# A two-layer attention trunk: q and k parts copied by DMA, dilated P scaled on ScalarE, differential P merged by one ratio

## The chip, the cores and the metric

The kernel runs on one core of a Trainium2 chip. The metric is device time in microseconds (us) of one execution. The core's engines are named as in the profile: PE (TensorE matmul), PEld (TensorE weight load), DVE (VectorE), ACT (ScalarE), POOL (GpSimd) and SP (SyncE, which here only issues DMAs). L12 is line 12 of the kernel before, unless another kernel is named.

## The reference

The input x is 512 tokens by 1024 channels, float32. There are two layers, each with the same parts:

```
h  = rms_norm(x) ;  u = h @ w_in                       # 1024 -> 10240
qa, ka, va, za, qb, kb, vb, zb, ga, gb = split(u)      # 1024 each
q, k of both branches: rotary turn of the first 16 of each head's 64 channels
branch A (16 heads of 64): softmax over three causal dilated windows, mixed by
    their softmax denominators                          # = one softmax with counts
branch B (8 heads, two q/k pairs of 64, v of 128):
    a = softmax(q1 k1) - lam * softmax(q2 k2) ; ob = rms_norm(a @ v) * (1 - lam_init)
ya = A * silu(za) ; yb = B * silu(zb)
x  = x + (sigmoid(ga) * (ya @ w_proj_a) + sigmoid(gb) * (yb @ w_proj_b)) @ w_out
```

A final rms_norm follows. All results are float32.

## The kernel before, in words

**Numbers.** Each float32 matrix product is made from two parts of each factor, a rounded high part and the remainder, and three matmuls: high by high, high by low, low by high. Whatever is to be multiplied is therefore first split, usually by one copy on ACT (the high part) and one subtraction on DVE (the low part). For the weights `split` (L99 to L103) does it, 1024 columns at a time.

**Projections.** Activations lie with channels on the 128 partitions and the 512 tokens along the row. `proj_T` (L268) makes one chunk of 256 output channels: 2 blocks `b` of 128, 8 steps `k` over the inputs, three 512-column matmuls per step (L282 to L284), into a PSUM tile `pj` of which there are three. At the end of a block an evacuation function is called. `proj_S` (L328) makes the two value projections of a layer with seven products instead of eight; its tiles X, Y, Z use the PSUM pools of scores, projections and transposes (two tiles, three and two).

**q and k.** A chunk ("qk", branch, u) holds 128 q channels (two heads, block 0) and the same 128 k channels (block 1). `ev_qk` (L398) evacuates a block: a shuffle on DVE (L401), a product with the cosine table on DVE (L403), a product with the sine table on POOL (L404), a sum on DVE (L405). Then the parts for the scores are made. The score matmuls (L480, L485, L486) contract over 128 partitions: 64 hold one part of a head's q, the other 64 the other part, and k is laid out so that two matmuls give all products. So each of the two heads needs its parts on both halves of the partitions; before, ACT and DVE write each half by instructions of 64 partitions by 512 columns (L410 to L413 for q, L419 to L422 for k).

**Dilated heads** (`a_pair`, L521, eight pairs a layer). For each half (one head): four score blocks (`s_steps`: matmuls, DVE adds the mask and takes the minimum at L487, ACT takes exp with its sum at L488); then `norm` multiplies the four blocks of 128, 256, 384 and 512 columns by the reciprocal sum on DVE (L528 to L531); `t_steps` transposes on PE (L506) and splits (L507 on ACT, L508 on DVE); `pv` multiplies with the values (L538).

**Differential heads** (`b_head`, L570, eight a layer). Two score maps P0 and P1 with their sums. `comb` (L575) forms P0/sum0 - lam * P1/sum1 with two DVE instructions per block (L582, L583). `pv` follows and collects the sums of squares (L605); after its second half the reciprocal root is taken (`inv_sqrt`, L238: DVE, then a power on POOL, L240), and four DVE instructions scale the output (L610); `turn` transposes it and multiplies with z (L618).

**z.** `ev_z` (L448) multiplies by the row scale `rb` on DVE (L453) and takes Silu on ACT. The first z chunk of a layer (`first`) runs before the row scales of the normalisation are known: at its last step `rstd_cols` and `layer_tables` make them, and then both blocks, which wait in the PSUM tiles of the scores, are evacuated (L287 to L291).

**Order.** Per layer: two z chunks, the value projection of A, the first q/k chunk, the value projection of B; then a merged list of `PARTS` (L886): chunks of q/k, z, the projection of A's result and the gates, with the steps of the heads laid between them by their nominal lengths (`merge`, L638). The steps of head u are paired with the value steps of head u-1 (`mix`). After that come the projection of B's result and the output projection. The instructions go to a planner in this order; it orders each engine's list by priority, which is the order of the program unless told otherwise, with a timing model for when operands and buffers are ready, and puts in all waits. Each engine then runs its list strictly in order.

**Buffers.** `b4` tiles (128 by 2 by 512) come from a pool of 29, which holds the normalised input, q and k parts, values, P, the branches' results and gates.

**DMA.** Weights come in chunks of 512 KB on SP's queue. POOL's queue carries 16 DMAs that add one half of a weight to another while loading (L112), all for the value projections. Values and projected results pass through device memory.

Of the kernel before, what the change touches and what calls it, by code (L numbers as in the profile page):

```python
# [16 lines left out]
P = 128  # L17
# [10 lines left out]
def bits(ap):  # L28
    return ap.bitcast(F32)
# [3 lines left out]
def trunk_kernel(ctx: ExitStack, tc: tile.TileContext, x, ws, norm_w, subln_w, final_w, lams, negb, rope, ident_in,  # L33
# [19 lines left out]
    def b4(name):  # L53
        return blk.tile([P, 2, T], F32R, tag="b4", name=name)
# [206 lines left out]
    def layer_tables():  # L261
        ps = rstd_rows()
        nc.scalar.activation(rb, ps, AF.Copy)
        nc.gpsimd.tensor_tensor(ct, rb, ct, OP.mult)
        nc.gpsimd.tensor_tensor(st, rb, st, OP.mult)


    def proj_T(what, rhs, evac, first=False):  # L268

        steps = []  # L270
        c, j0 = next_chunk(what)
        hold = {}

        def step(b, k):
            if b == 0 and k == 0:
                prep_to(j0 + 2)
            if k == 0:
                pool, tag = (pss, "s") if first else (psj, "pj")
                hold[b] = pool.tile([P, T], F32, tag=tag, name=f"pj{c}_{b}")
            ps, hb, o = hold[b], rhs(k), 256 * (k % 4) + b * P  # L280
            w_h, w_l = whi[j0 + k // 4][:, o:o + P], wlo[j0 + k // 4][:, o:o + P]
            nc.tensor.matmul(ps, w_h, hb[:, 0], start=(k == 0), stop=False)  # L282
            nc.tensor.matmul(ps, w_h, hb[:, 1], start=False, stop=False)  # L283
            nc.tensor.matmul(ps, w_l, hb[:, 0], start=False, stop=(k == 7))  # L284
            if b == 1 and k == 3:
                prep_to(j0 + 3)
            if k == 7 and first and b == 1:  # L287
                rstd_cols()
                layer_tables()
                for bb in range(2):  # L290
                    evac(bb, hold.pop(bb))  # L291
            if k == 7 and not first:
                evac(b, hold.pop(b))
        order = [(b, k) for k in range(8) for b in range(2)] if first else [(b, k) for b in range(2) for k in range(8)]
        for b, k in order:
            steps.append((683, lambda b=b, k=k: step(b, k)))
        return steps
# [97 lines left out]
    def hrhs(k):  # L395
        return st_["h"][k]

    def ev_qk(key):  # L398
        def f(b, ps):
            sw = t2(f"sw{key}{b}")  # L400
            nc.vector.stream_shuffle(sw, ps, SWAP)  # L401
            r = t2(f"rot{key}{b}")
            nc.vector.tensor_tensor(r, ps, ct, OP.mult)  # L403
            nc.gpsimd.tensor_tensor(sw, sw, st, OP.mult)  # L404
            nc.vector.tensor_tensor(r, r, sw, OP.add)  # L405
            lo, hi = slice(0, 64), slice(64, 128)
            if b == 0:
                qx = b4(f"qx{key}")

                nc.scalar.activation(qx[lo, 0], r[lo], AF.Copy, scale=-SCALE)  # L410
                nc.scalar.activation(qx[hi, 1], r[hi], AF.Copy, scale=-SCALE)
                nc.vector.scalar_tensor_tensor(qx[hi, 0], r[lo], -SCALE, bits(qx[lo, 0]), OP.mult, OP.subtract)
                nc.vector.scalar_tensor_tensor(qx[lo, 1], r[hi], -SCALE, bits(qx[hi, 1]), OP.mult, OP.subtract)  # L413
                st_["qk"][key] = [qx]
            else:

                for half, (mine, other) in enumerate(((lo, hi), (hi, lo))):
                    kx = b4(f"kx{key}{half}")
                    nc.scalar.activation(kx[mine, 1], r[mine], AF.Copy)  # L419
                    nc.vector.tensor_tensor(kx[mine, 0], r[mine], bits(kx[mine, 1]), OP.subtract)  # L420
                    nc.scalar.activation(kx[other, 0], bits(kx[mine, 1]), AF.Copy)
                    nc.vector.tensor_copy(kx[other, 1], bits(kx[mine, 0]))  # L422
                    st_["qk"][key].append(kx)
        return f

# [95 lines left out]
    def a_pair(layer, u):  # L521
# [4 lines left out]
        def norm(half):  # L526
            r = small.tile([P, 4], F32, tag="r", name=f"r{key}{half}")
            nc.vector.reciprocal(r, store["den", half])  # L528
            for i in range(4):
                p = store["p", half][i]  # L530
                nc.vector.tensor_scalar(p, p, r[:, i:i + 1], None, OP.mult)  # L531

        def pv(half):
            o = pso.tile([P, T], F32, tag="o", name=f"o{key}{half}")
# [35 lines left out]
    def b_head(layer, u):  # L570
# [2 lines left out]
        store = {}  # L573

        def comb():  # L575
            r = [small.tile([P, 4], F32, tag=f"rb{h}", name=f"rb{key}{h}") for h in range(2)]
            for h in range(2):
                nc.vector.reciprocal(r[h], store["den", h])
            nc.vector.tensor_scalar(r[1], r[1], nlam[:, layer:layer + 1], None, OP.mult)
            for i in range(4):  # L580
                p, p2 = store["p", 0][i], store["p", 1][i]
                nc.vector.tensor_scalar(p, p, r[0][:, i:i + 1], None, OP.mult)  # L582
                nc.vector.scalar_tensor_tensor(p, p2, r[1][:, i:i + 1], p, OP.mult, OP.add)  # L583

        def pv(half):

            ps = pso.tile([P, T], F32, tag="o", name=f"o{key}{half}")
            for n in range(2):
                i = 2 * half + n
                for j in range(i + 1):  # L590
                    v = store["v"][:, j]
                    for s in range(2):
                        nc.tensor.matmul(ps[:, 256 * n:256 * n + 256], pt_block(j, i, s), v,
                                         start=(j == 0 and s == 0), stop=(j == i and s == 1))
            if half == 0:
                store["o"] = tmp.tile([P, 4, P], F32, tag="t2", name=f"of{key}")
                store["ss"] = small.tile([P, 4], F32, tag="rs", name=f"rs{key}")
            o = store["o"][:, 2 * half:2 * half + 2]
            pp = ps.rearrange("p (n s d) -> p n s d", n=2, s=2)
            nc.scalar.activation(o, pp[:, :, 0], AF.Copy)  # L600
            nc.vector.tensor_tensor(o, pp[:, :, 1], o, OP.add)
            for n in range(2):
                i = 2 * half + n
                scr = small.tile([P, P], F32, tag="sqs", name=f"sqs{key}{i}", bufs=2)
                nc.scalar.activation(scr, o[:, n], AF.Square, accum_out=store["ss"][:, i:i + 1])  # L605
            if half == 1:
                r = store["ss"]
                inv_sqrt(r, r, 1.0 / P, 1e-5)
                for i in range(4):
                    nc.vector.tensor_scalar(store["o"][:, i], store["o"][:, i], r[:, i:i + 1], None, OP.mult)  # L610

        def turn():
            ps = pst.tile([P, T], F32, tag="t", name=f"ot{key}")
# [17 lines left out]
        def values(half):  # L631
            if half == 0:
                return t_steps((key, 0), store, 0) + [(900, lambda: pv(0)), (900, lambda: pv(1))]
            return [(430, turn)]
        return scores, values


# [356 lines left out]
```

## Time and profile before

| | |
|---|---|
| median of 3 runs | 1426.5 us (1426.38 to 1427.1) |
| the profiled execution | 1429.07 us |
| its span, first to last instruction | 1427.3 us |
| busy: PE, DVE, ACT, POOL | 1376.5, 1102.9, 879.0, 166.5 us |
| mean granted clock of TensorE | 0.989 |

A busy time is the union of an engine's instructions; instructions that only wait or issue on a queue are not in it. A group row of the profile has the line, the engine, the operation, output and inputs, shape, the count, then busy us and the mean ns of one, then idle time just before them and what ended it. A wait row has who waited, for whom, and us in total, times, longest. A timeline row has start us, length us, engine, line, and in brackets the idle time before it.

### The profile page before, as it was taken

What the parts mean: (1) busy time and instruction counts of PE and PEld (TensorE: products, weight loads), DVE (VectorE), ACT (ScalarE), POOL (GpSimd) and SP (SyncE); (2) the same over time, 40 slices, a digit from 0 to 9 for tenths busy, and PEclk for the clock granted to TensorE, in tenths of its full rate; (3) what the DMA queues carried; (4) which work ended last, traced back from release to release, by engine and by line L of the source; (5) the groups of instructions that cost most, each with busy time, mean ns of one, the idle gap of its engine ahead of it and who ended that gap; (6) DMA issues with size and microseconds to landing.
All of it is one profiled execution on the core that took longest, in us unless ns stands there. A gap on an engine that the chain in (4) does not pass through costs nothing.

```text
span 1427.3 us, 19038 instructions
## 1 busy us (share of the span) xinstructions
PE 1376.5 (96%) x6728; PEld 1144.1 (80%) x6728; DVE 1102.9 (77%) x2252; ACT 879.0 (62%) x1630; POOL 166.5 (12%) x139
## 2 busy tenths in 40 slices
PE   7999999999999999999999999999999999999998
PEld 5788777878788888888878887777878888888898
DVE  6876999999967898645466879999998688975554
ACT  8665667667665668632566666667766567774333
POOL 4100110110101120110220011010110011111000
PEclk9999999999999999999999999999999999999999
DMA  9643222212233323333585242212223322243421
GB/s 300 166 118 118 78 86 65 75 54 82 70 118 101 95 91 110 110 108 103 182 266 132 60 133 82 63 64 82 68 73 96 123 92 85 86 125 94 165 90 66
DMA packets 64607, 152.57 MB, mean 107 GB/s; under 512 B 6016, under 2 KB 22528, under 8 KB 64512
## 3 DMA queue, kind: packets, MB, share of 16 engines
q1 hardware_dynamic: 45312, 134.57, 29.4%
q0 software_dynamic: 2304, 8.39, 3.3%
q10 hardware_dynamic: 16896, 8.39, 2.0%
q8 instruction: 53, 0.87, 0.2%
q14 instruction: 42, 0.34, 0.1%
HBM read 134.55 MB, written 16.78 MB: 106 GB/s over the span
## 4 chain that ended last, share of the span: by engine, by line
PE 67%; DVE 19%; issue 7%; ACT 5%; DMA 1%; POOL 1%; SPq 0%; POOLq 0%; DVEq 0%; ACTq 0%
PE pj L282 16%; PE pj L283 16%; PE pj L284 16%; DVE wlo L103 3%; DVE pt L508 2%; PE X L303 1%; PE X L304 1%; PE X L302 1%; PE pv L302 1%; PE pv L304 1%; PE pv L303 1%; ACT whi L102 1%; DMA T<-ws_d 1%; PE Y L303 1%; POOL sq L206 1%
## 5 line engine op out<-in xcount | busy, mean ns | idle before, releaser
L282 PE MATMUL pj<-h,whi 128*128 128x512 f32 x1024 | 410.1, 402 | 15.0 <-DVE whi L801 6.5
L283 PE MATMUL pj<-h,whi 128*128 128x512 f32 x1024 | 408.0, 398 | 1.2 <-DVE h L189 1.1
L284 PE MATMUL pj<-h,wlo 128*128 128x512 f32 x1024 | 405.6, 398 | 0.0
L102 ACT ACTIVATE whi<-raw 128x1024 fp32r<-128x1024 f32 x207 | 218.7, 1057 | 173.2 <-PE pj L283 114.2
L103 DVE TENSOR_TENSOR wlo<-raw,whi 128x1024 fp32r<-128x1024 f32 x207 | 258.5, 1249 | 83.0 <-ACT whi L102 82.7
L282 PEld LDWEIGHTS pj<-h,whi 128*128 128x128 f32 x1024 | 195.5, 191 | 59.5 <-issue 6.4
L284 PEld LDWEIGHTS pj<-h,wlo 128*128 128x128 f32 x1024 | 195.3, 191 | 39.2 <-DVE wlo L103 0.3
L283 PEld LDWEIGHTS pj<-h,whi 128*128 128x128 f32 x1024 | 195.3, 191 | 39.1 <-DVE h L189 2.9
L103 DVE TENSOR_TENSOR wlo<-T,whi 128x1024 fp32r<-128x1024 f32 x24 | 31.2, 1300 | 14.9 <-ACT whi L102 14.8
L696 POOL TENSOR_TENSOR g<-g,pr 128x512 f32<-128x512 f32 x16 | 21.2, 1326 | 148.0 <-ACT g L695 148.0
L303 PE MATMUL pv<-wlo,mg 128*128 128x256 f32 x128 | 35.7, 283 | 0.0
L304 PE MATMUL pv<-whi,mg 128*128 128x256 f32 x128 | 35.7, 283 | 0.0
L302 PE MATMUL pv<-whi,mg 128*128 128x256 f32 x128 | 35.4, 283 | 0.0
L704 DVE TENSOR_TENSOR g<-pj,g 128x512 f32<-128x512 f32 x16 | 11.1, 692 | 30.5 <-PE pj L284 30.5
L102 ACT ACTIVATE whi<-T 128x1024 fp32r<-128x1024 f32 x24 | 25.1, 1055 | 8.6 <-PE pj L283 2.9
L206 POOL TENSOR_TENSOR sq<-sq,sq 128x512 f32<-128x512 f32 x12 | 19.7, 1638 | 88.6 <-issue 53.4
L708 ACT ACTIVATE mg<-g 128x512 fp32r<-128x512 f32 x16 | 10.1, 632 | 29.5 <-DVE g L705 29.5
L488 ACT ACT_TABLE_LOAD x21 | 26.9, 1283 | 0.3
L302 PE MATMUL X<-whi,h 128*128 128x512 f32 x64 | 24.1, 402 | 2.5 <-DVE z(0, 0, 0)_292 L453 2.5
L693 DVE TENSOR_TENSOR g<-pj,rb 128x512 f32<-128x512 f32 x32 | 22.0, 686 | 5.7 <-PE pj L284 5.6
L303 PE MATMUL X<-wlo,S 128*128 128x512 f32 x64 | 25.1, 393 | 0.8 <-DVE wlo L103 0.8
L303 PE MATMUL Y<-wlo,S 128*128 128x512 f32 x64 | 25.0, 391 | 0.8 <-DVE wlo L103 0.8
(4176 smaller groups left out, 3279.9 us busy)
## 6 DMA issues: line engine op xcount, KB each, us to landing
raw<-ws_d SPq DMA_DIRECT2D x199, 512.0 KB, 3.7
T<-ws_d POOLq DMA_DIRECT2D x16, 512.0 KB, 7.5
v_dram<-c ACTq DMA_DIRECT2D x24, 256.0 KB, 2.6
pa_dram<-pa SPq DMA_DIRECT2D x16, 256.0 KB, 3.1
pr<-pa_dram SPq DMA_DIRECT2D x16, 256.0 KB, 4.0
v_dram<-v ACTq DMA_DIRECT2D x8, 256.0 KB, 5.9
xr<-x_d SPq DMA_DIRECT2D x8, 256.0 KB, 4.4
x_dram<-xr SPq DMA_DIRECT2D x8, 256.0 KB, 3.2
```

What stands on the lines that cost most here:

```text
L102: nc.scalar.activation(whi[j], src, AF.Copy)
L103: nc.vector.tensor_tensor(wlo[j], src, bits(whi[j]), OP.subtract)
L206: nc.gpsimd.tensor_tensor(st_["acc"], st_["acc"], s, OP.add)
L282: nc.tensor.matmul(ps, w_h, hb[:, 0], start=(k == 0), stop=False)
L283: nc.tensor.matmul(ps, w_h, hb[:, 1], start=False, stop=False)
L284: nc.tensor.matmul(ps, w_l, hb[:, 0], start=False, stop=(k == 7))
L302: nc.tensor.matmul(ps, hh, w_h, start=first, stop=False, skip_group_check=True)
L303: nc.tensor.matmul(ps, hh, w_l, start=False, stop=False, skip_group_check=True)
L304: nc.tensor.matmul(ps, hl, w_h, start=False, stop=last, skip_group_check=True)
L488: nc.scalar.activation(p, p, AF.Exp, bias=mn[:, i:i + 1], scale=-1.0, accum_out=den[:, i:i + 1])
L508: nc.vector.tensor_tensor(dst[:, 1], ps[:, :n], bits(dst[:, 0]), OP.subtract)
L693: nc.vector.tensor_tensor(g[:, b], ps, rb, OP.mult)
```

## The change

Four edits, all in the functions above.

1. `ev_qk` no longer writes the halves by ACT and DVE. It makes one tile `hl` per block: the high part of all 128 partitions with one ACT copy, the low part with one DVE instruction. DMAs issued by POOL (`move`) then put the 64-partition pieces where the score matmuls want them: four for q (128 KB each), six for k (two of 256 KB, four of 128 KB).
2. `norm` of the dilated heads multiplies on ACT instead of DVE.
3. `comb` of the differential heads keeps P0 as it is and adds P1 times the ratio -lam * sum0/sum1, one DVE instruction a block. The missing factor 1/sum0 comes back as the scale of the squares (L605) and in the scaling of the output, which becomes one DVE instruction of 512 columns; root and scaling become steps of their own ahead of `turn`.
4. The row scales and the evacuation of the first z chunk are planned at high priority.

```
 proj_T:
             if k == 7 and first and b == 1:
-                rstd_cols()
-                layer_tables()
-                for bb in range(2):
-                    evac(bb, hold.pop(bb))
+                with tc.high_priority():
+                    rstd_cols()
+                    layer_tables()
+                    for bb in range(2):
+                        evac(bb, hold.pop(bb))
...
+    def move(to, of):
+        nc.gpsimd.dma_start(bits(to), bits(of))
 ev_qk:
+            hl = b4(f"hl{key}{b}")
+            f_ = -SCALE if b == 0 else 1.0
+            nc.scalar.activation(hl[:, 1], r, AF.Copy, scale=f_)
+            nc.vector.scalar_tensor_tensor(hl[:, 0], r, f_, bits(hl[:, 1]), OP.mult, OP.subtract)
             if b == 0:
                 qx = b4(f"qx{key}")
-                nc.scalar.activation(qx[lo, 0], r[lo], AF.Copy, scale=-SCALE)
-                nc.scalar.activation(qx[hi, 1], r[hi], AF.Copy, scale=-SCALE)
-                nc.vector.scalar_tensor_tensor(qx[hi, 0], r[lo], -SCALE, bits(qx[lo, 0]), OP.mult, OP.subtract)
-                nc.vector.scalar_tensor_tensor(qx[lo, 1], r[hi], -SCALE, bits(qx[hi, 1]), OP.mult, OP.subtract)
+                for half in range(2):
+                    mine = slice(64 * half, 64 * half + 64)
+                    move(qx[0:64, half], hl[mine, 1])
+                    move(qx[64:128, half], hl[mine, 0])
             else:
-                for half, (mine, other) in enumerate(((lo, hi), (hi, lo))):
+                for half in range(2):
                     kx = b4(f"kx{key}{half}")
-                    nc.scalar.activation(kx[mine, 1], r[mine], AF.Copy)
-                    nc.vector.tensor_tensor(kx[mine, 0], r[mine], bits(kx[mine, 1]), OP.subtract)
-                    nc.scalar.activation(kx[other, 0], bits(kx[mine, 1]), AF.Copy)
-                    nc.vector.tensor_copy(kx[other, 1], bits(kx[mine, 0]))
+                    mine = slice(64 * half, 64 * half + 64)
+                    move(kx[0:64], hl[mine])
+                    move(kx[64:128, 0], hl[mine, 1])
+                    move(kx[64:128, 1], hl[mine, 0])
...
 norm (a_pair):
-                nc.vector.tensor_scalar(p, p, r[:, i:i + 1], None, OP.mult)
+                nc.scalar.activation(p, p, AF.Copy, scale=r[:, i:i + 1])
...
 comb (b_head):
-            r = [small.tile([P, 4], F32, tag=f"rb{h}", name=f"rb{key}{h}") for h in range(2)]
-            for h in range(2):
-                nc.vector.reciprocal(r[h], store["den", h])
-            nc.vector.tensor_scalar(r[1], r[1], nlam[:, layer:layer + 1], None, OP.mult)
+            r = small.tile([P, 4], F32, tag="rb0", name=f"rb{key}")
+            q = small.tile([P, 4], F32, tag="rb1", name=f"rq{key}")
+            nc.vector.reciprocal(q, store["den", 1])
+            nc.vector.reciprocal(r, store["den", 0])
+            nc.vector.scalar_tensor_tensor(q, q, nlam[:, layer:layer + 1], store["den", 0], OP.mult, OP.mult)
+            store["r"] = r
             for i in range(4):
                 p, p2 = store["p", 0][i], store["p", 1][i]
-                nc.vector.tensor_scalar(p, p, r[0][:, i:i + 1], None, OP.mult)
-                nc.vector.scalar_tensor_tensor(p, p2, r[1][:, i:i + 1], p, OP.mult, OP.add)
+                nc.vector.scalar_tensor_tensor(p, p2, q[:, i:i + 1], p, OP.mult, OP.add)
...
 pv (b_head):
-                nc.scalar.activation(scr, o[:, n], AF.Square, accum_out=store["ss"][:, i:i + 1])
-            if half == 1:
-                r = store["ss"]
-                inv_sqrt(r, r, 1.0 / P, 1e-5)
-                for i in range(4):
-                    nc.vector.tensor_scalar(store["o"][:, i], store["o"][:, i], r[:, i:i + 1], None, OP.mult)
+                nc.scalar.activation(scr, o[:, n], AF.Square, scale=r, accum_out=store["ss"][:, i:i + 1])
+        def rms():
+            r = store["ss"]
+            inv_sqrt(r, r, 1.0 / P, 1e-5)
+        def scale():
+            r = store["ss"]
+            nc.vector.tensor_tensor(r, r, store["r"], OP.mult)
+            o = store["o"]
+            nc.vector.tensor_tensor(o, o, r.unsqueeze(2).to_broadcast([P, 4, P]), OP.mult)
...
-            return [(430, turn)]
+            return [(0, rms), (0, scale), (430, turn)]
```

More of the change, by code (lines that the diff above doesn't have):

```diff
@@ L405, in f @@
             nc.vector.tensor_tensor(r, r, sw, OP.add)
-            lo, hi = slice(0, 64), slice(64, 128)
+            hl = b4(f"hl{key}{b}")
+            f_ = -SCALE if b == 0 else 1.0
+            nc.scalar.activation(hl[:, 1], r, AF.Copy, scale=f_)
+            nc.vector.scalar_tensor_tensor(hl[:, 0], r, f_, bits(hl[:, 1]), OP.mult, OP.subtract)
             if b == 0:
                 qx = b4(f"qx{key}")
-                nc.scalar.activation(qx[lo, 0], r[lo], AF.Copy, scale=-SCALE)
-                nc.scalar.activation(qx[hi, 1], r[hi], AF.Copy, scale=-SCALE)
-                nc.vector.scalar_tensor_tensor(qx[hi, 0], r[lo], -SCALE, bits(qx[lo, 0]), OP.mult, OP.subtract)
-                nc.vector.scalar_tensor_tensor(qx[lo, 1], r[hi], -SCALE, bits(qx[hi, 1]), OP.mult, OP.subtract)
+                for half in range(2):
+                    mine = slice(64 * half, 64 * half + 64)
+                    move(qx[0:64, half], hl[mine, 1])
+                    move(qx[64:128, half], hl[mine, 0])
                 st_["qk"][key] = [qx]
             else:
-                for half, (mine, other) in enumerate(((lo, hi), (hi, lo))):
+                for half in range(2):
                     kx = b4(f"kx{key}{half}")
-                    nc.scalar.activation(kx[mine, 1], r[mine], AF.Copy)
-                    nc.vector.tensor_tensor(kx[mine, 0], r[mine], bits(kx[mine, 1]), OP.subtract)
-                    nc.scalar.activation(kx[other, 0], bits(kx[mine, 1]), AF.Copy)
-                    nc.vector.tensor_copy(kx[other, 1], bits(kx[mine, 0]))
+                    mine = slice(64 * half, 64 * half + 64)
+                    move(kx[0:64], hl[mine])
+                    move(kx[64:128, 0], hl[mine, 1])
+                    move(kx[64:128, 1], hl[mine, 0])
                     st_["qk"][key].append(kx)
@@ L603, in pv @@
                 i = 2 * half + n
+                r = store["r"][:, i:i + 1]
                 scr = small.tile([P, P], F32, tag="sqs", name=f"sqs{key}{i}", bufs=2)
-                nc.scalar.activation(scr, o[:, n], AF.Square, accum_out=store["ss"][:, i:i + 1])
-            if half == 1:
-                r = store["ss"]
-                inv_sqrt(r, r, 1.0 / P, 1e-5)
-                for i in range(4):
-                    nc.vector.tensor_scalar(store["o"][:, i], store["o"][:, i], r[:, i:i + 1], None, OP.mult)
+                nc.scalar.activation(scr, o[:, n], AF.Square, scale=r, accum_out=store["ss"][:, i:i + 1])
[7 more added lines that the diff above has]
+            nc.vector.tensor_tensor(o, o, r.unsqueeze(2).to_broadcast([P, 4, P]), OP.mult)
         def turn():
```

## The prediction

> **What bounds the kernel now.** I read the page first, then a table of five stretches, then PE's waits. The page:
>
> ```profile
> span 1427.3 us, 19038 instructions
> PE 1376.5 (96%) x6728; PEld 1144.1 (80%) x6728; DVE 1102.9 (77%) x2252; ACT 879.0 (62%) x1630; POOL 166.5 (12%) x139
> ```
>
> PE is busy 96% of the span, so at first sight there are only 51 us to win. But PE's busy time flatters: a 512-column matmul is shown with some 400 ns, while a clean stretch starts one every 222 ns (90 in 20 us), so a short stall disappears inside the neighbour's modelled length. The weight loads (PEld, one for each matmul) are the better measure of work done. The table by stretches (columns: stretch, length, then busy time and count of PE, PEld, DVE, ACT, POOL, then granted clock, DMA share, GB/s):
>
> ```profile
> 40.00:60.00 20.00, 18.56 (x75) 15.20 (x76) 16.02 (x28) 12.65 (x16) 0.89 (x1) 0.91 0.58 160
> ...
> 160.00:400.00 240.00, 225.62 (x1090) 183.42 (x1089) 223.68 (x518) 164.03 (x331) 24.37 (x19) 0.98 0.24 73
> ...
> 420.00:620.00 200.00, 199.04 (x997) 167.16 (x996) 153.07 (x353) 128.92 (x270) 25.16 (x21) 1.00 0.32 102
> ...
> 860.00:1100.00 240.00, 226.54 (x1095) 185.14 (x1094) 225.04 (x519) 164.16 (x330) 24.77 (x19) 0.97 0.25 76
> ...
> 1120.00:1320.00 200.00, 199.04 (x997) 167.15 (x996) 153.09 (x348) 127.23 (x267) 26.55 (x22) 1.00 0.32 100
> ```
>
> 160 to 400 us is the dilated branch of layer 0 with the first differential heads, 860 to 1100 the same of layer 1; there **DVE is 93% and 94% busy**, PE idles 14.4 and 13.5 us and the granted clock falls to 0.98 and 0.97. 420 to 620 and 1120 to 1320 are the differential heads: DVE 77%, PE idle under 1 us. Loads per us are 167.16/200 = 0.836 in the second kind and 183.42/240 = 0.764 and 185.14/240 = 0.771 in the first. At 0.836 the work of the dilated stretches would take 183.42/0.836 = 219.5 and 221.5 us: **20.5 and 18.5 us are lost, 39 together**. The mixes differ, so this is an estimate; its floor is the visible idle, 28 us. PE's waits name DVE:
>
> ```profile
> PE X L302 <- DVE z(0, 0, 0)_292 L453: 2.5, 1, 2.5
> PE o(1, 0, 0)1_7678 L538 <- DVE pt L508: 2.3, 1, 2.3
> ...
> PE pj L282 <- DVE rot(1, 0, 4)1_7988 L403: 1.2, 1, 1.2
> ```
>
> The dilated stage is therefore bound by DVE's queue, the rest by PE. An edit pays if it takes DVE work out of that stage.
>
> **The change, part by part.** What the removed instructions cost over the whole run; rows in this order: on DVE L412, L413 (q), L420, L422 (k), L531 (dilated normalisation), L582 and L610 (differential heads), then on ACT L410, L411, L419, L421. Columns as above with the one engine alone:
>
> ```profile
> 0.00:1427.30 1427.30, 21.92 (x32) 0.99 0.35 107
> 0.00:1427.30 1427.30, 24.34 (x32) 0.99 0.35 107
> 0.00:1427.30 1427.30, 45.40 (x64) 0.99 0.35 107
> 0.00:1427.30 1427.30, 29.80 (x64) 0.99 0.35 107
> 0.00:1427.30 1427.30, 42.66 (x128) 0.99 0.35 107
> 0.00:1427.30 1427.30, 21.23 (x64) 0.99 0.35 107
> 0.00:1427.30 1427.30, 16.00 (x64) 0.99 0.35 107
> 0.00:1427.30 1427.30, 19.95 (x32) 0.99 0.35 107
> 0.00:1427.30 1427.30, 20.18 (x32) 0.99 0.35 107
> 0.00:1427.30 1427.30, 40.31 (x64) 0.99 0.35 107
> 0.00:1427.30 1427.30, 40.46 (x64) 0.99 0.35 107
> ```
>
> And the nearest rows for what comes instead:
>
> ```profile
> L189 DVE SCALAR_TENSOR_TENSOR h<-xr,nw,h 128x512 fp32r<-128x512 f32 x8 | 6.0, 746 | 1.6 <-ACT h L188 1.6
> L708 ACT ACTIVATE mg<-g 128x512 fp32r<-128x512 f32 x16 | 10.1, 632 | 29.5 <-DVE g L705 29.5
> L429 ACT ACTIVATE c<-c,rstd 128x512 f32<-128x512 f32 x24 | 15.9, 711 | 0.7 <-DVE c L352 0.6
> L605 ACT ACTIVATE sqs(0, 1, 0)0_3481<-of(0, 1, 0)_3477 x1: 297/297/297, 399.3 to 399.3; 128x128 f32<-128x128 f32 x1
> L112 POOL DMA_DIRECT2D T<-ws_d x16 | 14.3, 916 | 55.4 <-ACT T L111 49.2 <-PE X L304 5.9 <-DVE S3f L225 0.3
> ```
>
> *q and k parts.* There are 32 q/k chunks. DVE per chunk: out 121.46/32 = 3.80 us, in two 128x512 subtractions at 0.746, so -2.30. ACT: out 120.9/32 = 3.78, in two at 0.632, so -2.51. Ten chunks fall into a dilated stretch: DVE -23.0, ACT -25.1 us.
>
> *Dilated normalisation.* Four DVE instructions per half head, 42.66/32 = 1.33 us, go to ACT. With a per-partition scale ACT takes 0.711 at 512 columns; at 128 columns I take 0.297 plus the 0.08 that separates 711 from 632, so 0.38; four widths average 0.545, 2.18 us a half. Fifteen halves per stretch: DVE -20.0, ACT +32.7. No table load comes with it, since the copies of L429 and L708 carry none.
>
> *Differential merge.* L582 goes: 21.23/16 = 1.33 us a head on DVE. L610's four multiplies (1.00 us a head) become one 128x512 (between 0.69 and 0.75) and a four-column one. Two merges fall into a stretch, -2.7; the other heads stand where DVE is only 77% busy and PE hides it: nothing.
>
> So a dilated stretch's DVE goes from 223.7 to 223.7-23.0-20.0-2.7 = **178**, its ACT from 164.0 to **171.6**. On a stretch of 220 us that is 81% and 78%: both near the 77% at which the differential stretch loses nothing, not at it. I give back a tenth of the 39 us, 4. Then PE's own work is late next.
>
> *The moves.* Each chunk adds 4 + 6 DMAs, issued on POOL. L112 is the only issue of that kind in the trace: 0.92 us, so 9.2 us a chunk; with two multiplies of 1.3 POOL gets 11.8 us a chunk, in a stretch of ten chunks 118 of 220. Landing is not shown for copies inside the chip's memory; bounds:
>
> ```profile
> T<-ws_d POOLq DMA_DIRECT2D x16, 512.0 KB, 7.5
> v_dram<-c ACTq DMA_DIRECT2D x24, 256.0 KB, 2.6
> ```
>
> A move carries 128 or 256 KB and adds nothing up, so 4 us, nearer the lower. From the end of the rotation to the first score a head then needs 0.63 + 0.75 + three issues (2.75) + 4 = 8.1 us. What it has, in the first and in the tightest case:
>
> ```profile
> 148.59 0.68 DVE L405 TENSOR_TENSOR rot(0, 0, 1)1_1232<-rot(0, 0, 1)1_1232,sw(0, 0, 1)1_1230 128x512 f32<-128x512 f32 x1
> ...
> 160.14 0.28 PE L480 MATMUL s(0, 0, 1)00_1265<-kx(0, 0, 1)0_1236,qx(0, 0, 1)_1159 128*128 128x256 f32 x1
> ```
> ```profile
> 516.75 0.68 DVE L405 TENSOR_TENSOR rot(0, 1, 6)1_4750<-rot(0, 1, 6)1_4750,sw(0, 1, 6)1_4748 128x512 f32<-128x512 f32 x1
> ...
> 524.75 0.28 PE L480 MATMUL s(0, 1, 6)00_4924<-kx(0, 1, 6)0_4754,qx(0, 1, 6)_4665 128*128 128x256 f32 x1
> ```
>
> 10.9 and 7.3 us. The same two rows of all 32 heads give 7 to 12 us for nine of them (mean 10) and over 15 for the others. So the tightest loses a little: 1 us a layer, 2 together. What hides the rest is projection matmuls between. Behind a move that waits for its source on POOL stand the next chunk's L404 multiply, for which L405 and then the PSUM tile wait, and in the differential heads L240's power; a chunk has over 20 us, so I cost that at nothing (if the cover goes: the rival below). Two more tiles of the 29-buffer pool live a few us per chunk; at nothing for the same reason.
>
> *A rule that speaks against it.* POOL's issue and DVE's work do overlap in the trace, and an elementwise POOL instruction does hold DVE:
>
> ```profile
> 29.01 1.28 DVE L225 TENSOR_TENSOR S3f<-x 128x512 f32<-128x512 f32 x2
> 29.36 1.83 POOL L112 DMA_DIRECT2D T<-ws_d  x2
> ```
> ```profile
> 210.34 1.28 POOL L404 TENSOR_TENSOR sw(0, 0, 4)1_1776<-sw(0, 0, 4)1_1776,st 128x512 f32<-128x512 f32 x1 [10.82 <-DVE sw(0, 0, 4)1_1776 L401]
> 210.81 1.36 DVE L413 SCALAR_TENSOR_TENSOR qx(0, 0, 4)_1686<-rot(0, 0, 4)0_1682,qx(0, 0, 4)_1686 64x512 fp32r<-64x512 f32 x1
> ```
>
> Two issues under two DVE additions: neither is longer (0.92 each, 1.28 for two). Under L404 a DVE instruction took 1.36, where the mean of its 32 is 24.34/32 = 0.76. So an elementwise POOL instruction costs DVE time and an issue costs it nothing here. The Trainium skill, "SBUF — State Buffer", section "SBUF: two separate sides", says that a DMA issued from POOL cannot write its descriptors while DVE runs a copy or a tensor-scalar in its two-port mode, and tells of a 620 ns transfer that took 3100 ns. By that an issue waits for such a DVE instruction and the time is that of rival (c), 1445; of these forms, though, L422, L531, L582 and L610 go with the change, and by the row above the sum stays.
>
> *First z.* PE's 2.5 us wait for L453, in the 40 to 60 stretch with the clock at 0.91:
>
> ```profile
> 33.38 0.58 ACT L263 ACTIVATE rb<-ps_rb 128x512 f32<-128x512 f32 x1
> ...
> 40.70 1.28 DVE L453 TENSOR_TENSOR z(0, 0, 0)_292<-pj,rb 128x512 f32<-128x512 f32 x2
> ...
> 41.44 0.50 PE L302 MATMUL X<-whi,h 128*128 128x512 f32 x1 [2.52 <-DVE z(0, 0, 0)_292 L453]
> ```
>
> Its scale is ready at 34.0 and DVE takes it at 40.7 behind other work. Put ahead, the 2.5 go, and some of the clock (20 x 0.09 = 1.8); the work now pushed back 1.3 us feeds PE too. Between 0 and 4.3; I take 3.
>
> **Sum.** 39 - 4 - 2 + 3 = 36, and 1 for the stretches' edges: 37. The profiled execution took 1429.07 us (span 1427.3 and 1.8 around it), 2.6 above the median 1426.5. 1429.07 - 37 - 2.6 = **1389.5, say 1390 us**.
>
> **Rivals.** (a) *ACT becomes the bound.* Normalisation now stands in ACT's queue between exp and the transposes, 0.85 us longer per half than on DVE and behind 1.06 us weight splits. For it: ACT at 78% serves PE's PSUM copies too. Against: it also loses 25 us. If each of 32 halves makes PE wait 0.6 us, 19 come back: 1409. (b) *PE's order, not DVE, sets the stage.* For it: PE's 96%, and single waits of 1 us and less. Against: two stretches of like work whose loss follows DVE's share. Then only z is won: 1424. (c) *Slower: the moves come late.* If an issue doubles to 1.8 us, as L413 did under L404, landing is 7.5 and one of q's moves still stands in front, a head needs 1.4 + 4 x 1.8 + 7.5 = 16.1 us; the nine tight heads lose 6.1 each, 55: 1390 + 55 = 1445. It decides from about 14.4 us a head on, where nine times 4.4 eats up the 37 and 2.9 more. For it: 320 issues where there were 16. Against: the 0.92 and the 2.6 rows. (d) *The change doesn't take DVE work out*, because L404 and the new 128-partition instructions hold each other; it is (b)'s time.
>
> **Numbers.** Forecast 58%, (a) 20, (b) with (d) 10, (c) 10, better than the range 2. The likeliest's own range: 1375 to 1402. The stalls hidden in PE's modelled length may be half as much again as the 39, so 58 won: 1429.07 - 58 - 3 - 2.6 = 1366, the low end. The high end takes in (a) and (b): 1424. A change under 0.2% (2.9 us) can't be told from none. Faster 0.80, same 0.09, slower 0.11.
>
> **What would show it.** Right: DVE under 85% and PE's loads above 0.82 a us in the dilated stretches, which end some 18 us earlier each; L112-like issues near 0.9 us, landing under 5; no wait of X for L453. Wrong: PE waits for kx or for a DMA at L480 (c), for ACT's p or pt (a), or DVE at 75% with PE's loads still at 0.77 (b).

## The result, and the profile after

| | before | after |
|---|---|---|
| median of 4 runs each on one chip | 1426.8 us (1426.38 to 1429.17) | 1391.96 us (1391.43 to 1392.57) |
| the profiled execution, its span | 1429.07, 1427.3 | 1392.57, 1390.8 |
| mean granted clock of TensorE | 0.989 | 0.994 |

The change takes 34.8 us: a ratio of 0.9753, 95% interval 0.9736 to 0.977. The forecast was 1390, with 37 us to be won. Line numbers from here on are those of the kernel after: the moves are issued at L400, the sine product is L408, the two halves `hl` are made at L415 (ACT) and L416 (DVE), `ev_z` multiplies at L461, the first score matmul is L488, the dilated normalisation is L539, and `t_steps` has L514 (PE), L515 (ACT) and L516 (DVE).

The page of the kernel after, its first lines and the queue that carries the moves (packets, MB, share of 16 engines):

```profile
span 1390.8 us, 19560 instructions
...
PE 1356.6 (98%) x6728; PEld 1138.8 (82%) x6728; DVE 971.6 (70%) x1900; ACT 859.2 (62%) x1630; POOL 335.7 (24%) x459
...
q0 software_dynamic: 19712, 58.74, 18.8%
```

DVE lost 131 us of work, ACT only 20, POOL gained 169; nearly all of that, 166.56 us, is the issuing of the moves, which does count in POOL's busy time. The table by stretches of the kernel after, with the columns of the prediction's first table; the second dilated stretch is read 20 to 40 us earlier, where its work now lies:

```profile
40.00:60.00 20.00, 19.01 (x77) 15.55 (x78) 15.99 (x28) 13.07 (x17) 0.88 (x1) 0.91 0.55 153
...
160.00:400.00 240.00, 236.14 (x1190) 197.75 (x1189) 192.36 (x436) 176.24 (x379) 76.19 (x118) 0.99 0.56 148
420.00:620.00 200.00, 200.00 (x993) 168.07 (x992) 133.12 (x276) 116.05 (x228) 47.67 (x61) 1.00 0.48 136
820.00:1080.00 260.00, 254.44 (x1281) 213.25 (x1280) 207.66 (x469) 189.15 (x405) 83.86 (x130) 0.99 0.57 149
1120.00:1320.00 200.00, 200.00 (x988) 167.54 (x988) 131.49 (x260) 112.88 (x211) 40.02 (x49) 1.00 0.45 134
```

In the dilated stretches PE's loads come at 197.75/240 = 0.824 and 213.25/260 = 0.820 a us, where they came at 0.764 and 0.771; DVE is 80% busy in both (192.36/240, 207.66/260), ACT 73% in both. The differential stretches run at 168.07/200 = 0.840 and 0.838, hardly above their 0.836.

Where the time came from is read by work done at fixed times. Weight loads alone (busy us and count), before:

```profile
0.00:400.00 400.00, 302.35 (x1726) 0.98 0.37 110
400.00:800.00 400.00, 332.15 (x1900) 1.00 0.42 128
800.00:1100.00 300.00, 234.27 (x1364) 0.98 0.26 80
```

and after:

```profile
0.00:400.00 400.00, 317.81 (x1835) 0.99 0.60 164
400.00:800.00 400.00, 332.32 (x1887) 1.00 0.50 143
800.00:1100.00 300.00, 246.86 (x1473) 0.99 0.55 147
```

By 400 us the kernel after is 317.81 - 302.35 = 15.46 us of loads ahead, and from 800 to 1100 it gains another 12.59; between, nothing (0.17). At 0.836 a us that is 18.5 us won in the dilated stretch of layer 0, 0.2 between and 15.1 in layer 1, 33.8 of the 36.5 us by which the span fell. But the busy time of the loads isn't quite a fixed measure either: the same 6728 loads take 1144.1 us before and 1138.8 after. Their number is fixed, so the time at which the n-th load starts places the whole difference (us from the start of the span):

| load | before | after | lead of after |
|---|---|---|---|
| 560th | 143.45 | 142.30 | 1.2 |
| 1680th | 389.61 | 368.76 | 20.9 |
| 3640th | 803.94 | 781.53 | 22.4 |
| 5040th | 1110.00 | 1070.04 | 40.0 |
| 6728th, the last | 1420.45 | 1379.58 | 40.9 |
| end of the span | 1427.26 | 1390.79 | 36.5 |

So 19.7 us are won in the dilated stretch of layer 0 and 17.6 in that of layer 1, 3.6 in all other stretches together, and **4.4 us are lost again behind the last load**. What differs there is a DRAIN instruction of POOL at the end of the program (the three drains of this line, shortest, median and longest in ns, before and after):

```profile
L989 POOLq DRAIN  x3: 40/102/1979, 1422.5 to 1427.0; - x3
```
```profile
L1005 POOLq DRAIN  x3: 46/93/8342, 1381.7 to 1390.5; - x3
```

The longest takes 8.34 us where it took 1.98, and the span ends 0.8 us behind it (before, 2.8 us). In all ten kernels of this record with ten moves a chunk on POOL's queue it takes 8.34 us, in the three without moves there 1.97 or 1.98. With twenty half moves a chunk it takes 4.84, so it doesn't simply grow with their number; why is open.

What PE waits for, the longest lines of the kernel after:

```profile
PE pj L282 <- DVE whi L817: 6.5, 1, 6.5
PE X L303 <- DVE z(0, 0, 0)_292 L461: 2.5, 1, 2.5
PE s(1, 0, 2)00_7759 L488 <- DMA kx(1, 0, 2)0_7658<-hl(1, 0, 2)1_7655: 1.7, 1, 1.7
```

The 2.3 us waits of `o` for `pt` are gone. A single head waits 1.7 us for a move. The wait of X for the first z is the same 2.5 us as before.

### The profile page after: what moved, and what is told of

Read it like the earlier page. It is cut to its first block, busy times and chain, and to the rows that moved or that the text cites. A ratio compares the mean times of both kernels' runs of the same rounds, so it can differ in the third digit from the quotient of the medians.

```text
span 1390.8 us, 19560 instructions
## 1 busy us (share of the span) xinstructions
PE 1356.6 (98%) x6728; PEld 1138.8 (82%) x6728; DVE 971.6 (70%) x1900; ACT 859.2 (62%) x1630; POOL 335.7 (24%) x459
## 4 chain that ended last, share of the span: by engine, by line
PE 91%; DVE 3%; DMA 2%; ACT 1%; issue 1%; POOL 1%; SPq 0%; POOLq 0%; DVEq 0%; ACTq 0%
PE pj L282 21%; PE pj L283 21%; PE pj L284 21%; PE X L304 2%; PE X L305 2%; PE X L303 2%; PE Y L304 1%; PE Y L305 1%; PE Y L303 1%; PE pv L303 1%; PE pv L305 1%; PE pv L304 1%; DMA T<-ws_d 1%; DMA kx(1, 0, 2)0_7658<-hl(1, 0, 2)1_7655 1%; DVE wlo L103 1%
## 5 line engine op out<-in xcount | busy, mean ns | idle before, releaser
L103 DVE TENSOR_TENSOR wlo<-raw,whi 128x1024 fp32r<-128x1024 f32 x207 | 264.8, 1280 | 103.8 <-ACT whi L102 103.3
L206 POOL TENSOR_TENSOR sq<-sq,sq 128x512 f32<-128x512 f32 x12 | 19.7, 1642 | 88.1 <-ACT sq L202 87.7
L103 DVE TENSOR_TENSOR wlo<-T,whi 128x1024 fp32r<-128x1024 f32 x24 | 29.3, 1224 | 15.2 <-ACT whi L102 15.1
L720 DVE TENSOR_TENSOR g<-pj,g 128x512 f32<-128x512 f32 x16 | 11.1, 692 | 30.5 <-PE pj L284 30.5
L102 ACT ACTIVATE whi<-T 128x1024 fp32r<-128x1024 f32 x24 | 25.2, 1056 | 10.8 <-DVE T L134 3.9
L112 POOL DMA_DIRECT2D T<-ws_d x16 | 14.6, 930 | 53.9 <-ACT T L111 43.3
L304 PE MATMUL X<-wlo,h 128*128 128x512 f32 x64 | 25.8, 403 | 0.4 <-DVE wlo L103 0.4
```

What stands on the lines that cost most here:

```text
L102: nc.scalar.activation(whi[j], src, AF.Copy)
L103: nc.vector.tensor_tensor(wlo[j], src, bits(whi[j]), OP.subtract)
L206: nc.gpsimd.tensor_tensor(st_["acc"], st_["acc"], s, OP.add)
L304: nc.tensor.matmul(ps, hh, w_l, start=False, stop=False, skip_group_check=True)
```

## The experiments

Each kernel ran on the same chip as a set of runs of the kernel before, whose median was 1426.8 to 1428.05 us; kernels are therefore compared by their ratios to it, and a difference of two ratios is turned into us at 1427. One interval is about plus or minus 2 us wide.

One thing is common to all of them. The planner makes new lists for each kernel: the matmuls are the same 6728, but 734 to 1287 of them stand at another place of PE's list than in the kernel after (111 with edit 4 undone), counted as those outside the longest part in common order. No run kept the order fixed, so a difference is that of the edit and of the new order together. A new order can be cheap: edit 3 undone moves 734 matmuls and costs nothing that can be told.

| kernel | median us | ratio to before (95%) | against after |
|---|---|---|---|
| after | 1391.96 | 0.9753 (0.9736 to 0.977) | |
| edit 1 undone | 1421.45 | 0.9962 (0.9947 to 0.9976) | +29.8 |
| edit 2 undone | 1394.31 | 0.9772 (0.9758 to 0.9787) | +2.7 |
| edit 3 undone | 1390.58 | 0.9746 (0.9731 to 0.976) | -1.0 |
| edit 4 undone | 1392.43 | 0.9759 (0.9742 to 0.9775) | +0.9 |
| DVE work added back | 1420.88 | 0.9945 (0.9929 to 0.9962) | +27.4 |
| ACT work added back | 1399.49 | 0.9802 (0.9787 to 0.9817) | +7.0 |
| both added back | 1418.13 | 0.993 (0.9911 to 0.9949) | +25.3 |
| moves in two | 1449.97 | 1.0153 (1.0138 to 1.0168) | +57.1 |
| moves on SP's queue | 1408.52 | 0.9874 (0.9847 to 0.9902) | +17.3 |
| norm on DVE, copy on ACT | 1456.47 | 1.0207 (1.0188 to 1.0226) | +64.8 |
| norm on ACT, copy on DVE | 1471.45 | 1.0312 (1.0298 to 1.0326) | +79.8 |
| first z put ahead by an edge, edit 3 undone | 1389.44 | 0.9736 (0.9723 to 0.9749) | -2.4 |

### Each edit undone

Edit 1 undone: `ev_qk` makes the halves by ACT and DVE as before, edits 2 to 4 stay.

```diff
-            hl = b4(f"hl{key}{b}")
-            nc.scalar.activation(hl[:, 1], r, AF.Copy, scale=f_)
-            nc.vector.scalar_tensor_tensor(hl[:, 0], r, f_, bits(hl[:, 1]), OP.mult, OP.subtract)
-            ... ten moves ...
+            # L410 to L413 and L419 to L422 of before
```

> The changed kernel with its first edit undone: the parts of q and k are again written by ACT and DVE instructions of 64 partitions, and no tile is moved by DMA. DVE theory (the dilated stretches were lengthened by DVE's queue): DVE gets 2.3 us a chunk back, 23 us in each dilated stretch, so its share there goes from 80% to some 90%, and about half of the 35 us come back: 1403 to 1414 us, PE's loads per us there near 0.79. Rival (the moves bring little and their lateness costs): the time stays at 1392 or falls to 1388, with DVE's share up and PE's loads per us unchanged.

1421.45 us: neither expectation held; nearly all of the gain, 29.8 of 34.8 us, goes with this one edit. By the count of loads it loses 15.8 and 15.1 us in the two dilated stretches, and wins the 4.4 us back at the end, since no move is on POOL's queue. Two windows of 220 us inside the dilated stretches, in the columns of the tables by stretches, for before, after and this kernel:

```profile
160.00:380.00 220.00, 206.91 (x1000) 168.37 (x999) 204.80 (x470) 148.08 (x293) 24.37 (x19) 0.98 0.23 69
840.00:1060.00 220.00, 207.41 (x1010) 169.60 (x1010) 206.53 (x472) 151.30 (x299) 23.71 (x19) 0.98 0.23 71
```
```profile
160.00:380.00 220.00, 216.15 (x1090) 181.17 (x1089) 178.26 (x404) 161.97 (x346) 75.15 (x117) 0.99 0.58 150
840.00:1060.00 220.00, 214.44 (x1081) 179.81 (x1080) 177.19 (x402) 161.04 (x343) 74.15 (x115) 0.99 0.57 147
```
```profile
160.00:380.00 220.00, 208.42 (x1026) 171.72 (x1024) 189.34 (x417) 177.90 (x361) 24.43 (x19) 0.99 0.23 72
840.00:1060.00 220.00, 210.42 (x1038) 174.00 (x1037) 190.38 (x422) 182.11 (x370) 26.04 (x21) 0.98 0.23 72
```

DVE stands at 86 and 87% there, between the 93 of before and the 81 of after, yet the loads go at 171.72/220 = 0.781 and 0.791, much nearer to before.

Edit 2 undone:

```diff
-                nc.scalar.activation(p, p, AF.Copy, scale=r[:, i:i + 1])
+                nc.vector.tensor_scalar(p, p, r[:, i:i + 1], None, OP.mult)
```

> The changed kernel with its second edit undone: the dilated P is again scaled on DVE. DVE theory: 20 us of DVE return to each dilated stretch and some 33 us of ACT leave it; about half of the 35 us come back, a little less than with the first edit undone: 1400 to 1412 us. Rival (ACT has become the bound after the change): taking 33 us from ACT gains as much as DVE loses, the time stays within 1389 to 1395.

1394.31 us, 2.7 above after, with overlapping intervals: not to be told from nothing. By the count of loads it loses 2.7 us in the dilated stretch of layer 0 and wins 1.8 in that of layer 1. The same two windows:

```profile
160.00:380.00 220.00, 213.32 (x1064) 177.94 (x1063) 193.09 (x452) 134.03 (x284) 76.61 (x117) 0.98 0.57 148
840.00:1060.00 220.00, 214.81 (x1092) 180.14 (x1091) 196.61 (x467) 138.25 (x294) 79.23 (x118) 1.00 0.57 149
```

DVE is 88 and 89% busy here, more than with edit 1 undone, and the loads go at 0.809 and 0.819. **DVE's share alone therefore doesn't set the rate.** ACT, at 61 and 63%, has 23 to 28 us less than after.

Edits 3 and 4 undone, each alone: `comb`, the squares and the scaling of the output as before; and the four lines of the first z chunk without the priority.

> The changed kernel with its third edit undone: the differential P is merged and its output scaled as before. DVE theory: the differential stretches have DVE to spare (77% before the change, with no PE loss), so this edit is worth nothing there and two merges in each dilated stretch: 1391 to 1395 us. Rival (every us of DVE counts): 2 us a head for 16 heads return, 1400 us and more.

> The changed kernel with its fourth edit undone: the row scales and the first z are planned at ordinary priority. The order of DVE's, ACT's and POOL's lists around the first z of layer 0 is the same with and without the edit, so the prediction's 3 us can't come from there: 1391 to 1394 us, and the 2.5 us wait of X for z stays. Rival (the edit acts through layer 1, where the lists do differ): 1394 to 1397 us.

1390.58 and 1392.43 us: neither edit is worth anything that these runs can tell. On edit 4 the trace shows a reason. First z of the kernel after:

```profile
32.96 0.57 ACT L263 ACTIVATE rb<-ps_rb 128x512 f32<-128x512 f32 x1
...
36.69 1.76 DVE L235 TENSOR_TENSOR S<-S2f,S 128x512 fp32r<-128x512 f32 x1
...
39.12 1.21 DVE L103 TENSOR_TENSOR wlo<-raw,whi 128x1024 fp32r<-128x1024 f32 x1
40.26 1.28 DVE L461 TENSOR_TENSOR z(0, 0, 0)_292<-pj,rb 128x512 f32<-128x512 f32 x2
```

Its scale is ready at 33.5 and DVE still takes it at 40.3, behind the sums S2 (L235) and weight splits, as before. The lists of DVE, ACT and POOL around the first z of layer 0 have the same order with and without the priority. That the planner takes the scale to be ready later than it is would explain it; this was not tried by itself. Nor is PE's wait for this z a fixed price of the order: with edit 4 undone DVE takes z at 41.1 us, later still, and PE waits 0.4 us for it, because it comes to X later; over the kernels here that keep this order the wait is 0.4 to 2.5 us.

### Work added back to the kernel after

Is it the amount of DVE work at the q/k evacuation, or the coupling of ACT and DVE there? Unused work was added behind `hl`, about as much as edit 1 takes away: three 128x512 additions a chunk on DVE (first kernel), four copies a chunk on ACT (second), both (third).

```diff
+            xd = t2(f"xd{key}{b}")
+            for _ in range(1 + b):
+                nc.vector.tensor_tensor(xd, r, r, OP.add)
```
```diff
+            xa = t2(f"xa{key}{b}")
+            for _ in range(1 + 2 * b):
+                nc.scalar.activation(xa, r, AF.Copy)
```

> The changed kernel with DVE work put back that computes nothing used: after the parts of q one extra 128x512 addition, after those of k two, 2.1 us a chunk, as much as the first edit took off DVE; they wait for the rotated block alone. Theory W (the amount of work on DVE's and ACT's lists decides): undoing the second edit also gave DVE 20 us a stretch and cost only 2.3 us while ACT was relieved, so 1395 to 1405 us. Theory C (not the amount, but the chain in which ACT and DVE waited for each other while they wrote the halves of q and k): at most 1396 us.

> The changed kernel with ACT work put back that computes nothing used: one extra 128x512 copy after the parts of q and three after those of k, 2.5 us a chunk, as much as the first edit took off ACT. Theory W: 1393 to 1403 us. Theory C: at most 1395 us.

> The changed kernel with both loads put back, on DVE and on ACT, independent of one another; q and k are still moved by DMA. This is the first edit's work without its chain. Theory W: the time returns to that of the kernel with the first edit undone, 1415 to 1425 us. Theory C: it stays within 1392 to 1402 us. In between, both count.

The DVE work alone brings back 27.4 us, more than either theory gave it; the ACT work 7.0; both together 25.3, not more than the DVE work alone. The added instructions over the whole run, on DVE in the first kernel and on ACT in the second, and then the first window of the three kernels in their order:

```profile
0.00:1419.20 1419.20, 68.52 (x96) 0.99 0.51 143
```
```profile
0.00:1400.90 1400.90, 79.11 (x128) 0.99 0.51 145
```
```profile
160.00:380.00 220.00, 208.28 (x1039) 172.10 (x1037) 192.64 (x416) 154.66 (x327) 76.50 (x119) 1.00 0.52 141
```
```profile
160.00:380.00 220.00, 213.27 (x1069) 177.72 (x1068) 175.37 (x403) 177.69 (x380) 76.48 (x119) 0.99 0.56 147
```
```profile
160.00:380.00 220.00, 211.41 (x1052) 174.73 (x1050) 194.58 (x420) 176.76 (x372) 76.12 (x119) 0.99 0.53 144
```

68.5 us of DVE work, 2.1 a chunk, costs 27.4 us with every move still in place; undoing edit 1, which by the prediction's 2.30 a chunk returns 74 us of it, and takes the moves away, costs 29.8. In the dilated stretches alone, by the count of loads, the added DVE work costs 11.4 and 12.9 us, edit 1 undone 15.8 and 15.1. So **DVE work at the evacuation of q and k, with the order that the planner gives it, brings back some four fifths of what edit 1 wins there** (24.3 of 30.9 us); the rest isn't attributed. The moves cost PE little on the way, 1.7 us of named waits in the kernel after, but 4.4 us at the end. The loads at 172.10/220 = 0.782 are those of edit 1 undone (0.781).

But the DVE work of this kernel (192.64 in the window) equals that of edit 2 undone (193.09), which is 24.7 us faster. Two things differ: ACT has 20 us less to do there, and the work stands at another place. The ACT kernels speak against the first being all: 79 us more on ACT cost only 7.0, and on top of the DVE work nothing (25.3 against 27.4), though ACT goes there from 154.66 to 176.76 us in the window. The next two kernels were to decide it.

### The place of the work

Edit 2 undone, with the same products also made on ACT into scratch; and the kernel after with the same products also made on DVE into scratch.

```diff
+                nc.vector.tensor_scalar(p, p, r[:, i:i + 1], None, OP.mult)
+                nc.scalar.activation(t2(f"xs{key}{half}{i}")[:, :p.shape[1]], p, AF.Copy, scale=r[:, i:i + 1])
```
```diff
                 nc.scalar.activation(p, p, AF.Copy, scale=r[:, i:i + 1])
+                nc.vector.tensor_scalar(t2(f"xs{key}{half}{i}")[:, :p.shape[1]], p, r[:, i:i + 1], None, OP.mult)
```

> The kernel with the second edit undone (normalisation on DVE, 1394 us) and in addition the same four products made on ACT into a scratch that nothing reads: ACT keeps the 33 us a dilated stretch that the edit gave it, DVE has its 20 us back. Theory W2 (a dilated stretch is lost when DVE is near 88% while ACT is over 70%, since PE's tiles pass through both, one after the other; undoing the second edit was cheap because it relieved ACT): 1412 to 1424 us. Theory P (it depends on where DVE's work stands: work right behind the rotation of q and k delays the release of PE's tile, work spread among the heads does not): 1394 to 1403 us.

> The changed kernel (normalisation on ACT) with the same four products made on DVE too, into a scratch that nothing reads: 20 us a dilated stretch on DVE, as much as the extra additions behind q and k that cost 29 us, but spread among the heads. Theory W2: 1412 to 1424 us. Theory P: 1392 to 1402 us.

1456.47 and 1471.45 us, far beyond both theories. First window of each:

```profile
160.00:380.00 220.00, 203.29 (x943) 165.23 (x944) 175.39 (x408) 145.24 (x303) 69.97 (x106) 0.94 0.47 125
```
```profile
160.00:380.00 220.00, 199.98 (x891) 160.01 (x892) 170.80 (x395) 139.34 (x294) 65.17 (x101) 0.91 0.42 115
```

DVE is *less* busy than in the kernel that each was made from (193.09 and 178.26), in the second ACT too (161.97), though work was added, and the granted clock falls to 0.94 and 0.91. The scratch product on one engine has to wait for the real one on the other, in a list kept in order, so these kernels added waits and not only work. They also take their scratch from the ten 128x512 buffers that the rotation of q and k uses. DVE's wait for ACT's half of the transposes, in the first of the two and in the kernel after:

```profile
DVE pt L516 <- ACT pt L515: 49.3, 45, 3.7
```
```profile
DVE pt L516 <- ACT pt L515: 21.7, 23, 1.7
```

They are inconclusive on place against amount. That a wait across two engines inside the normalisation costs more than its work would fit them, but the buffers and the new order were changed with it, so this is not shown.

### The moves

Each move in two, 20 issues a chunk instead of ten, half as large:

```diff
-        nc.gpsimd.dma_start(bits(to), bits(of))
+        for c in (slice(0, 256), slice(256, 512)):
+            nc.gpsimd.dma_start(bits(to[..., c]), bits(of[..., c]))
```

> The changed kernel with every move cut in two by columns: 20 issues a chunk on POOL instead of 10, at 0.52 us each 5.2 us more per chunk before the last part lands. The prediction's working (only the nine tight heads can be late): the tightest heads lose 1 to 3 us each, 1394 to 1408 us, with waits of the first score for a move of kx in the list of PE's waits. Rival (there is room everywhere, the moves are off the path): 1391 to 1394 us.

1449.97 us, 57 above after and slower than before; much more than expected. Issues at L400 over the run (L401 in the second) and landing, after and in two:

```profile
0.00:1390.80 1390.80, 166.56 (x320) 0.99 0.52 146
...
DMA to landing us min/median/max: 2.2/4.5/10.2
```
```profile
0.00:1447.80 1447.80, 341.23 (x640) 0.99 0.50 140
...
DMA to landing us min/median/max: 1.8/3.1/7.7
```

An issue takes 166.56/320 = 0.52 and 341.23/640 = 0.53 us; the half moves even land sooner. PE's waits in this kernel:

```profile
PE X L303 <- ACT whi L102: 8.4, 2, 4.2
...
PE ot(1, 1, 1)_10423 L632 <- DVE of(1, 1, 1)_10290 L627: 3.5, 1, 3.5
PE ot(0, 1, 1)_4037 L632 <- DVE of(0, 1, 1)_3904 L627: 3.4, 1, 3.4
PE s(1, 1, 0)00_9540 L489 <- DMA kx(1, 1, 0)1_9326<-hl(1, 1, 0)1_9316: 2.4, 1, 2.4
```

Only 4 us of PE's waits name a move (2.4, and 1.6 in layer 0). Two of 3.5 are heads whose output is scaled late; POOL's issues don't cause these, since POOL had stood idle for 27.7 and 25.2 us when the DVE step ahead of the power was done, and took the power at once. 8.4 are for weight splits on ACT. The planner's order is another one: 1287 matmuls are moved, and the first score of the first head starts at 142.5 us instead of 134.1. By the count of loads 8.4 us are lost ahead of the 560th load, 10.0 and 15.3 in the dilated stretches, 16.5 between them and 10.3 behind, and 3.5 are won at the end. So the loss is spread over the whole kernel, and its largest part isn't settled.

The moves on SP's queue, which otherwise carries the weights:

```diff
-        nc.gpsimd.dma_start(bits(to), bits(of))
+        nc.sync.dma_start(bits(to), bits(of))
```

> The changed kernel with the ten moves of a chunk issued on SP's queue instead of POOL's, where they stand among the weight loads. If POOL's issue time (0.52 us each) or the multiplies and powers queued behind the moves on POOL cost something: 1386 to 1391 us and POOL's busy time back under 180 us. If the moves' waits hold up the weight loads behind them on SP: over 1395 us, with waits for raw in the list of ACT's waits. If neither matters: 1391 to 1394 us.

1408.52 us (1404.05 to 1415.75), 17 above after, though POOL is back to 24 us of work in the first window. The profiled execution is the fastest of its four, 11.1 us behind that of after by its span; it loses 15.5 us up to the last load and wins 4.4 at the end. What SP's queue waits for; who waits for the moves; what PE waits for:

```profile
SPq L96 <- DVE wlo L103: 461.1, 89, 29.2
```
```profile
  DVE p(0, 1, 1)1_3584 L489: 4.8, 1
  DVE p(1, 1, 1)1_9810 L489: 3.3, 1
```
```profile
PE s(0, 1, 1)12_3625 L493 <- DVE rb(0, 1, 1)_3661 L588: 4.6, 1, 4.6
PE s(1, 1, 1)12_9851 L493 <- DVE rb(1, 1, 1)_9887 L588: 3.3, 1, 3.3
```

A weight load (L96) stands in that queue until its buffer is free, up to 29.2 us. That a move waited behind such a load isn't shown: the row would look alike without moves (31.3 us is its longest in the kernel after), and ACT's list names no wait for `raw`, which the expectation named as its sign. DVE stands 4.8 and 3.3 us before it can write a head's P, until a move is done, and PE's waits of 4.6 and 3.3 for the same two heads follow from it. In layer 0 the move is one of a later chunk's k, the last of which is issued by 370.2 us; DVE goes on at 376.2. That is 8 of the 15.5 us; what the rest waits for is not settled. The Trainium skill, "SBUF — State Buffer", section "Summary: rules for kernel authors", advises to issue from the ACT or SP queue a DMA that is to be hidden under DVE's work. Here that was the slower way by 17 us, though the moves landed in 3.6 us (median) instead of 4.5.

### A faster version

Edit 3 undone, and the splits of the sums S2 ordered behind the first z by an edge, where the priority had not moved them:

```diff
-            nc.vector.tensor_tensor(z[:, b], ps, rb, OP.mult)
+            st_["zi"] = nc.vector.tensor_tensor(z[:, b], ps, rb, OP.mult).ins
...
+            with tc.issue_after(st_["zi"]):
+                h_split(layer, ("S2",))
```

> A candidate to beat both kernels: the changed kernel with the third edit undone (1390.6 us measured), and with the splits of S2 put behind the first z on DVE's list by an ordering edge, so that the scores' PSUM tile of the first z is released earlier. The 2.5 us wait of X for z should shrink by 1 to 2 us in layer 0: 1387 to 1391 us. Rival (X then waits for the pushed-back S2 splits or for the weight split): 1390 to 1393 us.

1389.44 us over five runs (1388.63 to 1390.87), 0.9736 of before. DVE around the first z:

```profile
38.60 1.27 DVE L461 TENSOR_TENSOR z(0, 0, 0)_292<-pj,rb 128x512 f32<-128x512 f32 x2
39.80 1.28 DVE L235 TENSOR_TENSOR S<-S2f,S 128x512 fp32r<-128x512 f32 x2
```

z is taken 1.7 us sooner, S2 behind it, and PE's wait of X for z is gone. It beats the kernel before clearly. Against the kernel after it is 2.4 us faster and against edit 3 undone, from which it was made, 1.4; both intervals overlap with its own, so that the edge itself brings time is not shown.

## Why the prediction was right, and where not

**What bounds the kernel.** Right in the stage: nearly all of the gain lies in the two dilated stretches, 19.7 and 17.6 us by the count of loads, 37.3 where the prediction had 20.5 and 18.5 less the tenth and the late k, 33. The measure chosen, weight loads a us instead of PE's busy share, is what made the 39 us visible where the page shows PE 96% busy. The sum came closer than its terms: the dilated stretches gave 4.3 us more than forecast, and 4.4 were lost at the end of the program by a term that the prediction did not have. That these two cancel is luck. Elsewhere 3.6 us came where the sum had 4, but not by the first z, which had 3 of them.

**"An edit pays if it takes DVE work out of that stage"** is half right. It holds for the q/k evacuation (27.4 us for 68.5 us of work, with the new order that comes with it). It fails for the dilated normalisation: edit 2 takes as much off DVE in a stretch, some 20 us, and brings 2.7. By the prediction's own terms (23.0, 20.0 and 2.7 a stretch) edit 2 should have carried 20.0/45.7 of the 34.8 us, 15. The total came out because the 39 us were read from PE's rate and not built up from the edits. Why the same DVE time weighs ten times less at the normalisation stays open: relief of ACT, the place behind the rotation and the order that the planner makes are the candidates, and the two kernels meant to part the first two added waits of their own.

**The sizes.** DVE went to 80% (81 predicted) and ACT to 73% (78 predicted). The normalisation takes on ACT:

```profile
0.00:1390.80 1390.80, 61.64 (x128) 0.99 0.52 146
```

1.93 us a half instead of 2.18. An issue takes 0.52 us; the 0.92 of the prediction is that of a row whose DMA adds while it loads 512 KB. Landing takes 4.5 instead of 4. These errors cancel for a head: 0.63 + 0.75 + three issues of 0.52 + 4.5 = 7.4 us instead of 8.1. The late k cost 1.7 us in one head; 2 were predicted. What the moves would do to the end of the program, 4.4 us, was not in the sum.

**First z, the term that failed.** Three us were put in for a wait that did not go. The prediction took "planned at high priority" for "placed ahead"; the lists show that it was not. An edge does place it ahead, but what that brings, 1.4 us against the kernel it was made from, can't be told from nothing. The wait itself is no fixed 2.5 us: it is 0.4 to 2.5 in kernels with the same order.

**The rivals.** (a) ACT as the bound fell: 79 us more on ACT cost 7.0, and edit 2 undone, which takes 61.64 us off ACT, is not faster. (b) fell with the loads' rate. (c), late moves, did not happen with ten issues a chunk; with 20 the kernel is slower than before, but waits for moves are 4 us of its loss, so most of it is not what (c) describes. (d) fell: DVE's busy time dropped by 131 us.

**The rule.** The Trainium skill's "SBUF — State Buffer", section "SBUF: two separate sides", would have POOL's issues held while DVE runs in its two-port mode. With DVE 80% busy in the dilated stretches the issues average 0.52 us, and with the added work, DVE 88% in the first window, 167.98 us for 320, the same:

```profile
0.00:1419.20 1419.20, 167.98 (x320) 0.99 0.51 143
```

With edit 2 undone, where DVE has its 128 tensor-scalar products back, they take 167.90. Nothing of such a hold is to be seen at the issue; in which mode DVE ran these instructions no trace shows. No run here shows whether the spread of the landing, 2.2 to 10.2 us, has to do with it.

## What to carry to other kernels

Measure a stage by the rate at which the bound engine completes a fixed kind of instruction, against a clean stretch of the same kernel; that gave the size of the gain where the busy share hid it. Afterwards, compare the times at which the n-th of them starts up to the end of the program: a cost behind the last one shows nowhere else. Don't divide such a gain among edits by the busy time that each removes: undo them one at a time, because 20 us of the same engine's work were worth some 12 us a stretch at one place and hardly one at another. A priority given to a planner is a wish; look in the lists whether the order changed. And an edit given to a planner is never alone: it comes with a new order, whose price only a run at a fixed order could part from it.

## What was not expected of the hardware

Twice the number of half-size moves landed sooner (median 3.1 against 4.5 us) at 0.53 us an issue, and still the kernel lost 57 us. Freeing POOL of its 166.56 us of issues by moving them to SP cost 17 us. With the moves on POOL's queue the program ends on a drain of 8.34 us instead of 1.98, 4.4 us later behind the last load. And two kernels with the same DVE busy time in the bound stretch (192.6 and 193.1 of 220 us) ended 24.7 us apart.
